# Recurrence steps of two head pairs and 128 tokens in place of one pair and 256

## The chip, the cores and the metric

The kernel runs on one core of a Trainium2 chip. The metric is the device time of one execution in microseconds (us), lower is better. The core has five engines that run side by side, each through its own instructions in order: PE (TensorE, matrix products), DVE (VectorE), ACT (ScalarE), POOL (GpSimd) and SP (SyncE, which here only issues DMAs). A matrix product needs a weight load ahead of it; the profile lists those as PEld.

## What is computed

Two layers of a decoder over 1024 tokens of width 1024. The even layer is an S5 state space model beside differential attention, the odd layer is RWKV-7 time mixing, and each layer ends with a SwiGLU feed-forward network (FFN). The change is in the RWKV-7 part alone:

```python
def rwkv7_recurrence(r, decay, k, v, kk, a):   # 16 heads of 64, 1024 tokens
    def step(state, inp):                      # state: 64 x 64 per head
        r_t, w_t, k_t, v_t, kk_t, b_t = inp
        sa = jnp.einsum('bhvk,bhk->bhv', state, -kk_t)
        state = (state * w_t[:, :, None, :] + sa[..., None] * b_t[:, :, None, :]
                 + v_t[..., None] * k_t[:, :, None, :])
        return state, jnp.einsum('bhvk,bhk->bhv', state, r_t)
    xs = (r, decay, k, v, kk, kk * a)          # along the tokens
    _, ys = lax.scan(step, s0, xs)
...
r = xr @ w_r;  k = xk @ w_k;  v = xv @ w_v     # 1024 x 1024 each
a = jax.nn.sigmoid(a0 + (xa @ a1) @ a2)
y = group_norm(rwkv7_recurrence(...)) + bonus
return (y * g) @ w_o
```

## The kernel before

The tokens are cut into two blocks of 512. For each block `rwkv_proj` computes k, r and v and puts them into DRAM (`kd`, one plane of 128 channels, so two heads, per head pair j = 0 to 7). `rwkv_algebra` then does the recurrence of the block in 16 steps of one head pair and TR = 256 tokens, and `rwkv_wo` multiplies by `w_o`. A step's 256 tokens are CR = 4 chunks of 64. Inside a chunk the token by token recurrence is replaced by products of 64 x 64 matrices, so that only the state (64 x 64 per head) goes from chunk to chunk.

A step goes through four stages, each a Python generator that yields between pieces of its work. `rwkv_prep` loads k, r, v (tiles `ks`, `rr`, `RV`), makes decays and keys from them (`pz` and `pa` are two small products with low-rank weights `wa2`, `FS` and `AR` its results) and ends with eight products `pA` that DVE masks into `AT`, `ZB` and `AR`. `rwkv_inv` inverts a triangular matrix per chunk by doubling, with PE and DVE in turn (`X`, `XE`, `QE`, `XF`), which gives `TT`. `rwkv_rec` is the recurrence over the chunks. `rwkv_out` normalises, multiplies with the gate and stores `z` to DRAM (`zd`).

`lockstep` runs four stages of four successive steps together: in each round every stage goes on by one yield, in the order out, rec, inv, prep. I call one run of `lockstep` a superstep; a block has 19. `weave` puts the FFN of another block between the rounds as filler: `RATE` = 2 times three products of 128 x 512 (L466, tiles `pg`, `pu`, `pd`) after every round. The order on PE is the order in which the code is written. The order on the other engines is set by a scheduler that simulates the kernel when it is built.

In `rwkv_rec` each chunk has three phases that hang on one another, and one yield stands between two of them. Phase one: PE multiplies with the state (`pR`, L1651, and the first half of the output, `pY`, L1653), DVE copies the result from PSUM (`Pb`, L1657). Phase two: one product with `TT` (L1660), ACT copies one half of it and DVE the other into `XU` (L1661, L1662). Phase three: PE makes the state's increment (L1666) and the rest of the output (L1668), DVE updates the state (L1673). So a superstep has twelve phases one after the other, and with its boundary 13 rounds.

The state itself stays in `Hc` between steps. The steps go over the pairs first, then over the tokens, so a pair's state is needed again eight steps later.

Of the kernel before, what the change touches and what calls it, by code (L numbers as in the profile page):

```python
# [12 lines left out]
AF = mybir.ActivationFunctionType  # L13
# [133 lines left out]
class Trunk:  # L147
# [1258 lines left out]
    def rwkv_prep(self, q, j, st):  # L1406


        nc = self.nc
        ap, pr, vec = self.ap, self.pr, self.vec  # L1410
        v, g_, s_ = nc.vector, nc.gpsimd, nc.scalar
        sl = slice(j * P, (j + 1) * P)
        tok = slice(q * TR, (q + 1) * TR)
        tw, ta = (a[:, (q * TR) % TB : (q * TR) % TB + TR] for a in (self.tw, self.ta))
# [3 lines left out]
        def t(tag, bufs=1, shape=None):  # L1418
            return ap.tile(shape or [P, TR], F32, tag=tag, name=self.nm(tag), bufs=bufs)
# [11 lines left out]
        nc.tensor.matmul(pz, lhsT=wa2, rhs=tw, start=True, stop=True)  # L1431
# [3 lines left out]
        s_.activation(lwt, pz, AF.Tanh, bias=vec[:, 0, j : j + 1], scale=0.5)  # L1435
# [20 lines left out]
        v.scalar_tensor_tensor(kk, ks, self.col("od_k_k", j), rn, op0=M, op1=M)  # L1456
# [4 lines left out]
        s_.activation(fk, at, AF.Identity, bias=vec[:, 2, j : j + 1], scale=vec[:, 3, j : j + 1])  # L1461
# [28 lines left out]
        AT, ZB = t("AT", 2, [P, CR, 64]), self.ZB[(8 * q + j) % 3]  # L1490
# [39 lines left out]
    def rwkv_inv(self, q, j, st):  # L1530
# [95 lines left out]
        for h in range(2):  # L1626
            s_.copy(XH[h][rows[h], 0, :], self.Hc[rows[h], j, :])
# [3 lines left out]
    def rwkv_rec(self, q, j, st):  # L1631
# [12 lines left out]
        def pt(tag, shape, bufs):  # L1644
            return pr.tile(shape, F32, tag=tag, name=self.nm("p" + tag), bufs=bufs)

        py = pt("Y", [P, CR, 64], 1)
        for c in range(CR):
            pp = pt("R", [P, 64], 1)
            for h in range(2):  # L1650
                te.matmul(pp[rows[h], :], lhsT=AR[h][:, c, 0:64], rhs=XH[h][:, c, :], start=True, stop=True)  # L1651
            for h in range(2):
                te.matmul(  # L1653
                    py[rows[h], c, :], lhsT=XH[h][:, c, :], rhs=AR[h][:, c, 64:128], start=True, stop=False, skip_group_check=True
                )
# [15 lines left out]
            for h in range(2):
                dst = XH[h][rows[h], c + 1, :] if c < CR - 1 else Hc[rows[h], j, :]
                v.scalar_tensor_tensor(dst, XH[h][rows[h], c, :], wc[rows[h], c : c + 1], ph[rows[h], :], op0=M, op1=AD)  # L1673
            if c < CR - 1:
                yield
# [4 lines left out]
    def rwkv_out(self, q, j, st):  # L1680
# [3 lines left out]
        sg = self.sg[:, (q * TR) % TB : (q * TR) % TB + TR]  # L1684
# [27 lines left out]
        te.matmul(pg, lhsT=g2w, rhs=sg, start=True, stop=True)  # L1712
        z = bo
        v.tensor_tensor(z, y1, pg, op=M)
        nc.sync.dma_start(self.zd[j][:, q * TR : (q + 1) * TR], z)
        yield

    def run(self):
# [46 lines left out]
        if mix1:  # L1765
            self.close(self.cq)
            self.mix1_open()
            drain(self.some(ps["v"], 16))
# [8 lines left out]
            drain(self.some(ps1["v"], 16))  # L1777
# [86 lines left out]
```

## Time and profile before

| | |
|---|---|
| median of 3 runs | 3177.56 us (3169.1 to 3178.48) |
| profiled execution, its own time | 3189.24 us |
| its span, first to last instruction | 3187.3 us |
| mean granted TensorE clock | 0.965 of 2.4 GHz |
| PE busy | 2976.2 us, 93% of the span |
| PEld / DVE / ACT / POOL busy | 71% / 60% / 37% / 28% |
| algebra of block 0, inside | 1264 to 1690 us |
| algebra of block 1, inside | 2110 to 2540 us |

The profile is of one execution, whose time lies a little above the median of the three timed runs. Lines such as L1666 are those of the kernel before. Products overlap in PE's pipeline, so the cost of one product in a series is the distance between the starts of two successive ones and not its own duration. One product in 32-bit floats shows as two matmul records; a row of "x4" is two products then. The filler's products show as one record each, about 0.23 us from start to start.

### The profile page before, as it was taken

The page shows a single profiled execution, that of the slowest core. Times are in us where ns is not written, and L with a number is a line of the kernel's source. Part 1 is how long each engine was busy: PE and PEld are TensorE (multiplying, and loading weights), DVE is VectorE, ACT ScalarE, POOL GpSimd, SP SyncE. Part 2 cuts the span into 40 slices and gives each one's busy share as a digit, 9 for nine tenths or more (in the row PEclk, how much of TensorE's full clock was granted, in tenths as well). Part 3 has the DMA queues.
Part 4 walks back from the last instruction along what each step waited for, and adds up shares of the span by engine and source line. Part 5 has one row for each costly group of instructions (what it writes and reads, how often), then busy time and mean ns, then how long its engine had stood idle before and what let it go on. Part 6 is the DMA issues. An engine that isn't in the chain of part 4 may idle for free.

```text
span 3187.3 us, 50746 instructions
## 1 busy us (share of the span) xinstructions
PE 2976.2 (93%) x19326; PEld 2250.0 (71%) x19326; DVE 1921.7 (60%) x3982; ACT 1193.9 (37%) x2446; POOL 889.5 (28%) x1007
## 2 busy tenths in 40 slices
PE   4879989999999998999999999989999999999999
PEld 1678866776777766677666777666776677777777
DVE  7744645555674645777777545467777874434443
ACT  3212334333223644444444345544444443322222
POOL 6562402000110302344434342024344444200000
PEclk7989978999999999999999999999999999999999
DMA  6853221223573444212222244522222213533332
GB/s 242 213 134 67 69 71 53 80 73 105 179 232 113 156 146 126 71 56 77 74 67 80 81 148 136 155 85 75 70 60 81 75 59 93 167 90 93 96 103 93
DMA packets 489857, 338.39 MB, mean 106 GB/s; under 512 B 44280, under 2 KB 451088, under 8 KB 488592
## 3 DMA queue, kind: packets, MB, share of 16 engines
q1 hardware_dynamic: 474288, 304.75, 32.2%
q0 software_dynamic: 7632, 25.68, 2.6%
q10 hardware_dynamic: 7696, 4.74, 0.6%
q8 instruction: 153, 2.51, 0.3%
q14 instruction: 88, 0.72, 0.1%
HBM read 292.63 MB, written 42.47 MB: 105 GB/s over the span
## 4 chain that ended last, share of the span: by engine, by line
PE 72%; DVE 12%; issue 6%; DMA 5%; ACT 3%; POOL 2%; SPq 0%; ACTq 0%; DVEq 0%; POOLq 0%
PE pg L466 13%; PE pu L466 13%; PE pd L466 12%; PE pkrv L466 8%; PE pout L466 5%; PE pq L466 3%; PE sps L1001 3%; DMA mwt<-in_w_ada 2%; PE po L1044 1%; ACT whi L449 1%; PE pR L1666 1%; PE pA L1592 1%; PE pR L1651 1%; PE pA L1495 1%; DVE wlo L450 1%
## 5 line engine op out<-in xcount | busy, mean ns | idle before, releaser
L449 ACT CAST whi<-wraw 128x1024 fp32r<-128x1024 f32 (+2 forms) x472 | 401.9, 852 | 887.7 <-PE pg L466 186.3
L466 PE MATMUL pd<-dd,whi 128*128 128x512 f32 x1408 | 463.3, 410 | 14.8 <-DVE x L534 10.7
L450 DVE TENSOR_TENSOR wlo<-wraw,whi 128x1024 fp32r<-128x1024 f32 (+2 forms) x288 | 296.1, 1029 | 271.9 <-ACT whi L449 255.4
L450 POOL TENSOR_TENSOR wlo<-wraw,whi 128x1024 fp32r<-128x1024 f32 (+2 forms) x184 | 326.0, 1773 | 461.5 <-ACT whi L449 420.1
L466 PE MATMUL pg<-fhi,whi 128*128 128x512 f32 x704 | 301.5, 428 | 13.0 <-DVE sg L521 10.8
L466 PEld LDWEIGHTS pd<-dd,whi 128*128 128x128 f32 x1408 | 254.0, 189 | 80.6 <-ACT whi L449 19.3
L466 PE MATMUL pu<-fhi,whi 128*128 128x512 f32 x704 | 295.4, 420 | 1.4 <-ACT ev L1365 0.8
L466 PE MATMUL pg<-fhi,wlo 128*128 128x512 f32 x704 | 283.4, 403 | 6.3 <-DVE wlo L450 6.3
L466 PE MATMUL pu<-fhi,wlo 128*128 128x512 f32 x704 | 279.1, 396 | 3.7 <-POOL wlo L450 2.2
L466 PE MATMUL pg<-flo,whi 128*128 128x512 f32 x704 | 281.7, 400 | 0.0
L466 PE MATMUL pd<-dd,wlo 128*128 128x512 f32 x704 | 279.4, 397 | 2.1 <-DVE oss L1053 0.9
L466 PE MATMUL pu<-flo,whi 128*128 128x512 f32 x704 | 277.7, 394 | 0.0
L534 DVE SCALAR_TENSOR_TENSOR x<-pd,mod,x 128x512 f32<-128x512 f32 x192 | 143.4, 747 | 122.9 <-PE pd L466 121.9
L466 PE MATMUL pkrv<-xh,whi 128*128 128x512 f32 x384 | 165.4, 431 | 12.3 <-ACT ev L1365 6.4
L466 PEld LDWEIGHTS pg<-fhi,whi 128*128 128x128 f32 x704 | 135.2, 192 | 47.2 <-DVE sg L521 12.0
L466 PEld LDWEIGHTS pg<-fhi,wlo 128*128 128x128 f32 x704 | 135.1, 192 | 40.3 <-DVE wlo L450 8.7
L466 PEld LDWEIGHTS pd<-dd,wlo 128*128 128x128 f32 x704 | 133.0, 189 | 38.8 <-DVE wlo L450 3.8
L466 PEld LDWEIGHTS pu<-fhi,whi 128*128 128x128 f32 x704 | 132.9, 189 | 36.3 <-issue 2.4
L466 PEld LDWEIGHTS pu<-fhi,wlo 128*128 128x128 f32 x704 | 132.6, 188 | 35.7 <-POOL wlo L450 3.0
L466 PE MATMUL pkrv<-xh,wlo 128*128 128x512 f32 x384 | 154.6, 403 | 1.3 <-DVE wlo L450 1.3
L466 PE MATMUL pkrv<-xl,whi 128*128 128x512 f32 x384 | 154.4, 402 | 0.0
L466 PEld LDWEIGHTS pg<-flo,whi 128*128 128x128 f32 x704 | 135.3, 192 | 25.3
(460 smaller groups left out, 6084.1 us busy)
## 6 DMA issues: line engine op xcount, KB each, us to landing
wraw<-in_ffn_w_gate SPq DMA_DIRECT2D x88, 512.0 KB, 3.7
wraw<-in_ffn_w_up SPq DMA_DIRECT2D x88, 512.0 KB, 3.8
wraw<-in_ffn_w_down SPq DMA_DIRECT2D x128, 256.0 KB, 2.7
mwt<-in_w_ada POOLq DMA_DIRECT2D x48, 512.0 KB, 5.4
mwt<-in_w_ada SPq DMA_DIRECT2D x32, 512.0 KB, 5.4
wraw<-in_ffn_w_down SPq DMA_DIRECT2D x64, 192.0 KB, 2.5
kd<-ev SPq DMA_DIRECT2D x48, 256.0 KB, 2.0
xs<-x SPq DMA_DIRECT2D x8, 1024.0 KB, 6.3
```

What stands on the lines that cost most here:

```text
L449: nc.scalar.copy(hi, raw)
L450: (eng or nc.vector).tensor_tensor(lo, raw, hi.bitcast(F32), op=ALU.subtract)
L466: nc.tensor.matmul(out, lhsT=w(k), rhs=x(k), start=first and i == 0, stop=last and i == n - 1)
L534: nc.vector.scalar_tensor_tensor(x[:, n, :], pd, gate[:, n : n + 1], x[:, n, :], op0=ALU.mult, op1=ALU.add)
L1001: nc.tensor.matmul(sp[:, c0 : c0 + n], lhsT=qT[r : r + 64, hd, o : o + P], rhs=kT[r : r + 64, hd % 2, c0 : c0 + n], start=True, stop=not l ...
L1044: nc.tensor.matmul(po, lhsT=wt[:, j - j0, :], rhs=vt[:, j, P * (hd % 2) : P * (hd % 2) + P], start=(j == 0), stop=(j == i))
L1495: nc.tensor.matmul(pas[h][:, c, :], lhsT=FS[rows[h], c, :], rhs=AR[h][rows[h], c, :], start=True, stop=True)
L1592: te.matmul(px[32 * g : 32 * g + 32], lhsT=XF[:, g, :], rhs=QE[:, g], start=True, stop=True)
L1651: te.matmul(pp[rows[h], :], lhsT=AR[h][:, c, 0:64], rhs=XH[h][:, c, :], start=True, stop=True)
L1666: te.matmul(ph[rows[h], :], lhsT=BE[:, c, rows[h]], rhs=XU[h][:, c, :], start=True, stop=True)
```

## The change

One step takes two neighbouring pairs (2j and 2j + 1) and 128 tokens in place of one pair and 256. A step still has four chunks of 64 tokens, now two of each pair, and all tiles keep their size of 256 columns (`u = 2 e + c` is chunk c of pair e). The recurrence goes in two rounds over c, and each round carries a chunk of both pairs in every phase. Between two phases stand two yields in place of one (`self.wait(2)`).

What depends on the pair (weights and per-channel factors) is done once for each of the two pairs on 128 columns: the products `pz`, `pa`, `pbn` and `pg`, four activations in `rwkv_prep` and one in `rwkv_out`, the product `kk` on DVE and `Brk` on POOL. The loads of k, r, v and the store of `z` take two planes in rows of 512 bytes in place of one in rows of 1 KB. `rr` and `wa2` have one buffer in place of two. A pair's state comes back after four steps.

```diff
@@ rwkv_algebra
-                    q, j = divmod(16 * b + s - d, 8)
+                    q, j = divmod(16 * b + s - d, 4)
@@ rwkv_prep
-        ks, rr, RV = t("ks"), t("rr", 2), t("RV", 4, [P, 2, TR])
+        pairs = [(2 * j + e, slice(e * P, (e + 1) * P)) for e in range(2)]
+        ks, rr, RV = t("ks"), t("rr"), t("RV", 4, [P, 2, TR])
         for d, dst in ((0, ks), (1, rr), (2, RV[:, 1, :])):
-            nc.sync.dma_start(dst, self.kd[d, j][:, tok])
-        wa2 = t("wa2", 2, [P, P])
+            nc.sync.dma_start(e2(dst), self.kd[d, 2 * j : 2 * j + 2].rearrange("e p t -> p e t")[:, :, tok])
+        wa2 = t("wa2", 1, [P, 2 * P])
...
-        nc.tensor.matmul(pz, lhsT=wa2, rhs=tw, start=True, stop=True)
+        for _, o in pairs:
+            nc.tensor.matmul(pz[:, o], lhsT=wa2[:, o], rhs=tw, start=True, stop=True)
...
-        s_.activation(lwt, pz, AF.Tanh, bias=vec[:, 0, j : j + 1], scale=0.5)
+        for i, o in pairs:
+            s_.activation(lwt[:, o], pz[:, o], AF.Tanh, bias=vec[:, 0, i : i + 1], scale=0.5)
...
@@ rwkv_inv
-            s_.copy(XH[h][rows[h], 0, :], self.Hc[rows[h], j, :])
+            s_.copy(XH[h][rows[h], 0::2, :], self.Hc[rows[h], 2 * j : 2 * j + 2, :])
@@ rwkv_rec
+        def units(c):
+            return [(e, 2 * e + c, h) for e in range(2) for h in range(2)]
...
-        for c in range(CR):
-            pp = pt("R", [P, 64], 1)
-            for h in range(2):
-                te.matmul(pp[rows[h], :], lhsT=AR[h][:, c, 0:64], rhs=XH[h][:, c, :], start=True, stop=True)
+        for c in range(2):
+            pp = pt("R", [P, 2, 64], 1)
+            for e, u, h in units(c):
+                te.matmul(pp[rows[h], e, :], lhsT=AR[h][:, u, 0:64], rhs=XH[h][:, u, :], start=True, stop=True)
...
-            Pb = t("Pb", [P, 64], 2)
+            Pb = t("Pb", [P, 2, 64])
             v.tensor_copy(Pb, pp)
-            yield
-            pu = pt("R", [P, 64], 1)
-            te.matmul(pu, lhsT=TT[:, c, :], rhs=Pb, start=True, stop=True)
-            s_.copy(XU[0][rows[0], c, :], pu[rows[0], :])
-            v.tensor_copy(XU[1][rows[1], c, :], pu[rows[1], :])
-            yield
+            yield from self.wait(2)
+            pu = pt("R", [P, 2, 64], 1)
+            for e in range(2):
+                te.matmul(pu[:, e, :], lhsT=TT[:, 2 * e + c, :], rhs=Pb[:, e, :], start=True, stop=True)
+            s_.copy(XU[0][rows[0], c::2, :], pu[rows[0]])
+            v.tensor_copy(XU[1][rows[1], c::2, :], pu[rows[1]])
+            yield from self.wait(2)
...
@@ run
-            drain(self.some(ps["v"], 16))
+            drain(self.some(ps["v"], 20))
```

The first place is on PE, late in a superstep of block 0. Before, a round holds the product of phase two (L1660) and the next one its phase three (L1666, L1668), with six products of filler between:

```order
L1660 MATMUL pR_16353<-Pb_16312,TT_10249 128x64
L1622 MATMUL pA_16357<-QE_16316,XF_16323 32x128 x2
L466 MATMUL pg_16349<-fhi_10338,whi_16345 128x512
L466 MATMUL pg_16349<-flo_10340,whi_16345 128x512
L466 MATMUL pg_16349<-fhi_10338,wlo_16346 128x512
L466 MATMUL pg_16349<-fhi_10338,whi_16345 128x512
L466 MATMUL pg_16349<-flo_10340,whi_16345 128x512
L466 MATMUL pg_16349<-fhi_10338,wlo_16346 128x512
L1666 MATMUL pR_16373<-XU_3377_15391,BE_15605 64x64
L1666 MATMUL pR_16373<-XU_3378_15392,BE_15605 64x64
L1668 MATMUL pY_15956<-ZB_10247,XU_3377_15391 64x64
L1668 MATMUL pY_15956<-ZB_10247,XU_3378_15392 64x64
```

Now phase three (L1685, L1687 of the new code) carries four units, and the round ahead of it ends with the last product `pA` of the preparation (L1508), while phase two stands a round earlier still, out of sight above the first row:

```order
L1508 MATMUL pA_16648<-AR_3610_16583,FS_16577 128x128
L466 MATMUL pg_16552<-fhi_10359,whi_16548 128x512
L466 MATMUL pg_16552<-flo_10361,whi_16548 128x512
L466 MATMUL pg_16552<-fhi_10359,wlo_16549 128x512
L466 MATMUL pg_16552<-fhi_10359,whi_16548 128x512
L466 MATMUL pg_16552<-flo_10361,whi_16548 128x512
L466 MATMUL pg_16552<-fhi_10359,wlo_16549 128x512
L1685 MATMUL pR_16666<-XU_3396_15743,BE_15941 64x64
L1685 MATMUL pR_16666<-XU_3397_15744,BE_15941 64x64
L1685 MATMUL pR_16666<-XU_3396_15743,BE_15941 64x64
L1685 MATMUL pR_16666<-XU_3397_15744,BE_15941 64x64
L1687 MATMUL pY_16283<-ZB_10245,XU_3396_15743 64x64
```

What moved: phases two and three of a chunk lie twelve filler products and one more group of other products apart, where it was six.

The second place is on DVE at the same point. Before, the copy `XU` (L1662), for which phase three waits, stands behind the six masks of the preparation (L1498), one FFN update and `AC`:

```order
L1657 COPY Pb_21999<-pR_21994 128x64
L1612 TENSOR_TENSOR QE_22003<-pA_22001,cstt 128x256
L1498 TENSOR_TENSOR AT_22012<-pA_22013,cstt 64x256
L1498 TENSOR_TENSOR ZB_10245<-pA_22013,cstt 64x256
L1498 TENSOR_TENSOR AR_4976_21930<-pA_22013,cstt 64x512
L1498 TENSOR_TENSOR AT_22012<-pA_22014,cstt 64x256
L1498 TENSOR_TENSOR ZB_10245<-pA_22014,cstt 64x256
L1498 TENSOR_TENSOR AR_4977_21931<-pA_22014,cstt 64x512
L534 SCALAR_TENSOR_TENSOR x_4365_19583<-pd_21990,mod_119,x_4365_19583 128x512
L1568 SCALAR_TENSOR_TENSOR AC_22105<-AT_22012,cstt 128x128
L1662 COPY XU_4756_21091<-pR_22032 64x64
L1625 COPY TT_10248<-pA_22036 32x4x32
```

Now the copy (L1681) stands ahead of the masks (L1511), and with the inversion's `X` behind the burst of the preparation (`y`, `ksq`, `AR`, `FS`: L1468 to L1485):

```order
L1601 TENSOR_TENSOR QE_21004<-pA_20999,cstt 128x256
L1468 SCALAR_TENSOR_TENSOR y_4600_21006<-ks_20737,vc_103,hbc_20978 128x128 x2
L1471 SCALAR_TENSOR_TENSOR ksq_21009<-at_20830,y_4600_21006 128x256
L1485 SCALAR_TENSOR_TENSOR AR_4605_21021<-y_4600_21006,Wx_20795 64x4x64
L1485 SCALAR_TENSOR_TENSOR AR_4606_21022<-y_4600_21006,Wx_20795 64x4x64
L1481 SCALAR_TENSOR_TENSOR FS_21016<-ksq_21009,L_20788 64x4x64 x2
L1606 TENSOR_TENSOR X_20730<-X_20730,pA_21041 128x4x16
L1681 COPY XU_4400_20223<-pR_21036 64x2x64
L1615 TENSOR_TENSOR XE_21047<-X_20730,cstt 128x256
L1617 STREAM_TRANSPOSE X_4611_21049<-X_20730 128x128
L1625 TENSOR_TENSOR QE_21076<-pA_21074,cstt 128x256
L1511 TENSOR_TENSOR AT_21085<-pA_21086,cstt 64x256
```

What moved: `XU` from behind the masks to a place ahead of them, one copy for two units.

## Rows read from the trace of the kernel before

**Rows 1.** By stretch: length; busy PE, PEld, DVE, ACT, POOL; clock; DMA share, GB/s.

```profile
1264.00:1690.00 426.00, 404.03 (x3644) 294.78 (x3644) 320.47 (x824) 181.90 (x473) 179.35 (x178) 0.99 0.24 70
...
2110.00:2540.00 430.00, 407.64 (x3670) 297.82 (x3670) 323.05 (x829) 183.11 (x475) 179.36 (x179) 0.99 0.23 69
```

**Rows 2.** PE's waits, whole span: us in total, times, longest us.

```profile
PE pR L1666 <- DVE XU L1662: 26.3, 30, 2.8
...
PE pA L1585 <- DVE Pb L1657: 7.1, 9, 1.5
...
PE pA L1585 <- DVE XE L1577: 3.0, 9, 0.7
```

**Rows 3.** PE in time: start, us, line, product, records [idle before, its end].

```profile
1383.42 0.48 PE L1666 MATMUL pR<-XU,BE 128*64 128x64 f32 x4 [2.76 <-DVE XU L1662]
...
1469.27 0.34 PE L1666 MATMUL pR<-XU,BE 128*64 128x64 f32 x4 [0.69 <-DVE XU L1662]
...
1613.71 0.34 PE L1666 MATMUL pR<-XU,BE 128*64 128x64 f32 x4 [1.63 <-DVE XU L1662]
```

**Rows 4.** DVE in order of time, a superstep's end.

```profile
1424.66 0.68 DVE L1498 TENSOR_TENSOR AR<-pA,cstt 64x512 f32<-64x512 f32 x1
...
1425.93 0.33 DVE L1568 SCALAR_TENSOR_TENSOR AC<-AT,cstt 128x128 f32<-128x128 f32 x1
1426.29 0.23 DVE L1662 COPY XU<-pR 64x64 f32<-64x64 f32 x1
...
1429.04 1.13 DVE L1577 TENSOR_TENSOR XE<-X,cstt 128x256 f32<-128x256 f32 x1
```

**Rows 5.** PE in order of time, 1418 to 1435 us.

```profile
1418.39 0.71 PE L1483 MATMUL pv<-cstt,RV 128*128 128x128 f32 x4
1418.86 0.71 PE L466 MATMUL pd<-dd,whi 128*128 128x512 f32 x2
1419.41 0.40 PE L466 MATMUL pd<-dd,wlo 128*128 128x512 f32 x1
...
1423.91 0.33 PE L1660 MATMUL pR<-Pb,TT 128*128 128x64 f32 x2
1424.17 0.41 PE L1622 MATMUL pA<-QE,XF 128*32 128x128 f32 x4
...
1426.58 0.34 PE L1666 MATMUL pR<-XU,BE 128*64 128x64 f32 x4 [0.40 <-DVE XU L1662]
1426.74 0.29 PE L1668 MATMUL pY<-ZB,XU 128*64 128x64 f32 x4
1426.96 0.73 PE L466 MATMUL pd<-dd,whi 128*128 128x512 f32 x2
1427.53 0.40 PE L466 MATMUL pd<-dd,wlo 128*128 128x512 f32 x1
1427.76 0.63 PE L466 MATMUL pd<-dd,whi 128*128 128x512 f32 x2
...
1429.63 0.39 PE L466 MATMUL pd<-dd,wlo 128*128 128x512 f32 x1
1429.94 0.34 PE L1651 MATMUL pR<-XH,AR 128*64 128x64 f32 x4
...
1433.31 0.70 PE L1446 MATMUL pa<-lta,wa 128*128 128x256 f32 x2
1433.66 0.81 PE L466 MATMUL pd<-dd,whi 128*128 128x512 f32 x2
1434.31 0.39 PE L466 MATMUL pd<-dd,wlo 128*128 128x512 f32 x1
```

**Rows 6.** PE's weight loads in order of time, the loads of one of these groups.

```profile
1418.39 0.52 PEld L1483 LDWEIGHTS pv<-cstt,RV 128*128 128x128 f32 x4
```

**Rows 7.** DVE's groups of instructions, 1264 to 1690 us: busy us, mean ns.

```profile
L1662 DVE COPY XU<-pR 64x64 f32<-64x64 f32 x47 | 10.7, 228 | 2.0 <-ACT XU L1661 0.5
...
L1673 DVE SCALAR_TENSOR_TENSOR Hc<-XH,wc,pR 64x64 f32<-64x64 f32 x22 | 6.1, 279 | 0.8
```

More of the change, by code (lines that the diff above doesn't have):

```diff
@@ L1445, in rwkv_prep @@
         pa = pr.tile([P, TR], F32, tag="k", name=self.nm("pa"))
-        nc.tensor.matmul(pa, lhsT=wa2, rhs=ta, start=True, stop=True)
+        for _, o in pairs:
+            nc.tensor.matmul(pa[:, o], lhsT=wa2[:, o], rhs=ta, start=True, stop=True)
         yield
         at = t("at")
-        s_.activation(at, pa, AF.Tanh, bias=vec[:, 1, j : j + 1], scale=0.5)
+        for i, o in pairs:
+            s_.activation(at[:, o], pa[:, o], AF.Tanh, bias=vec[:, 1, i : i + 1], scale=0.5)
         ksq = t("ksq")
-        s_.activation(ksq, ks, AF.Square, scale=self.col("od_k_k", j))
+        for i, o in pairs:
+            s_.activation(ksq[:, o], ks[:, o], AF.Square, scale=self.col("od_k_k", i))
         yield
@@ L1455, in rwkv_prep @@
         kk = t("y1")
-        v.scalar_tensor_tensor(kk, ks, self.col("od_k_k", j), rn, op0=M, op1=M)
+        for i, o in pairs:
+            v.scalar_tensor_tensor(kk[:, o], ks[:, o], self.col("od_k_k", i), rn[:, o], op0=M, op1=M)
         bt = t("ksq")
@@ L1460, in rwkv_prep @@
         fk = t("kr")
-        s_.activation(fk, at, AF.Identity, bias=vec[:, 2, j : j + 1], scale=vec[:, 3, j : j + 1])
+        for i, o in pairs:
+            s_.activation(fk[:, o], at[:, o], AF.Identity, bias=vec[:, 2, i : i + 1], scale=vec[:, 3, i : i + 1])
         k2 = t("lwt")
@@ L1488, in rwkv_prep @@
         yield
-        AT, ZB = t("AT", 2, [P, CR, 64]), self.ZB[(8 * q + j) % 3]
+        AT, ZB = t("AT", 2, [P, CR, 64]), self.ZB[(4 * q + j) % 3]
         msk = self.cst("tri").rearrange("p (o n) -> p o n", o=1)
@@ L1668, in rwkv_rec @@
+            s_.copy(XU[0][rows[0], c::2, :], pu[rows[0]])
+            v.tensor_copy(XU[1][rows[1], c::2, :], pu[rows[1]])
+            yield from self.wait(2)
+            ph = pt("R", [P, 2, 64], 1)
+            for e, u, h in units(c):
+                te.matmul(ph[rows[h], e, :], lhsT=BE[:, u, rows[h]], rhs=XU[h][:, u, :], start=True, stop=True)
+            for e, u, h in units(c):
                 te.matmul(
-                    py[rows[h], c, :], lhsT=XU[h][:, c, :], rhs=ZB[:, h, c, :], start=False, stop=True, skip_group_check=True
+                    py[rows[h], u, :], lhsT=XU[h][:, u, :], rhs=ZB[:, h, u, :], start=False, stop=True, skip_group_check=True
@@ L1670, in rwkv_rec @@
                 )
[L1671 to L1675, printed above, removed]
+            for e, u, h in units(c):
+                dst = Hc[rows[h], 2 * j + e, :] if c else XH[h][rows[h], u + 1, :]
+                v.scalar_tensor_tensor(dst, XH[h][rows[h], u, :], wc[rows[h], u : u + 1], ph[rows[h], e, :], op0=M, op1=AD)
@@ L1676, in rwkv_rec @@
+            if not c:
+                yield from self.wait(2)
         st["ys"] = ys = t("ys", [P, TR])
@@ L1683, in rwkv_out @@
         ap, pr = self.ap, self.pr
-        sg = self.sg[:, (q * TR) % TB : (q * TR) % TB + TR]
+        sg = self.sg[:, (q * P) % TB : (q * P) % TB + P]
+        pairs = [(2 * j + e, slice(e * P, (e + 1) * P)) for e in range(2)]
         v, g_, s_, te = nc.vector, nc.gpsimd, nc.scalar, nc.tensor
@@ L1703, in rwkv_out @@
         v.tensor_tensor(y1, ys, rb, op=M)
-        s_.activation(y1, y1, AF.Identity, bias=self.col("od_ln_b", j), scale=self.col("od_ln_g", j))
+        for i, o in pairs:
+            s_.activation(y1[:, o], y1[:, o], AF.Identity, bias=self.col("od_ln_b", i), scale=self.col("od_ln_g", i))
         pbn = pr.tile([P, TR], F32, tag="y", name=self.nm("pR"))
-        te.matmul(pbn, lhsT=Brk, rhs=RV[:, 0, :], start=True, stop=True)
+        for _, o in pairs:
+            te.matmul(pbn[:, o], lhsT=Brk[:, o], rhs=RV[:, 0, o], start=True, stop=True)
         bo = yq
@@ L1711, in rwkv_out @@
         pg = pr.tile([P, TR], F32, tag="y", name=self.nm("pR"))
-        te.matmul(pg, lhsT=g2w, rhs=sg, start=True, stop=True)
+        for _, o in pairs:
+            te.matmul(pg[:, o], lhsT=g2w[:, o], rhs=sg, start=True, stop=True)
         z = bo
         v.tensor_tensor(z, y1, pg, op=M)
-        nc.sync.dma_start(self.zd[j][:, q * TR : (q + 1) * TR], z)
+        nc.sync.dma_start(
+            self.zd[2 * j : 2 * j + 2].rearrange("e p t -> p e t")[:, :, q * P : (q + 1) * P], z.rearrange("p (e t) -> p e t", e=2)
+        )
         yield
@@ L1776, in run @@
             fs, fs1 = {}, {}
-            drain(self.some(ps1["v"], 16))
+            drain(self.some(ps1["v"], 20))
             if ffn1:
```

25 lines of the change are left out of this document (12 added, 13 removed).

## The prediction

> **What bounds the kernel now.** I first read the busy time by stretch [rows 1]. In the algebra of both blocks PE is busy 404.03 of 426 us and 407.64 of 430 us, at a granted clock of 0.99 (the 2.4 GHz level). PE is the bound there, and it is idle for 22 us in each stretch, 44 us in all. DVE is second with 320.47 us, 75%. ACT (181.90 us) and POOL (179.35 us) have room, and so have the DMAs (share 0.24). So the change can gain in two ways only: fewer or cheaper products on PE, and less idle time of PE. The filler is only shifted: six filler products fewer stand in each superstep (72 in place of 78 in PE's order) and follow after the algebra instead.
>
> Next I read who PE waits for [rows 2]. The longest wait of the kernel is the one that the change is about: L1666, phase three of a chunk, waits for the DVE copy `XU`, 26.3 us in 30 waits. Two waits of the inversion follow (L1585 behind `Pb` and `XE`): 7.1 + 3.0 = 10.1 us in 18 waits. The first of them is named after `Pb`, but L1585 does not read `Pb`; `XE` stands next to it in DVE's queue.
>
> Then I looked at where in the superstep the 30 waits lie, by their distance from `pz`, which opens it. There are four places, and the same ones come back in both blocks: 5 to 6 us after `pz` (8 waits, 4.9 us, such as the one at 1469.27), 14.7 us (2 waits, 3.3 us, the one at 1613.71), 21 to 23 us (8 waits, 10.9 us, the longest of them 2.76 us at 1383.42) and 29 to 33 us (12 waits, 7.2 us, such as 0.40 us at 1426.58) [rows 3, 5]. The last place shows the cause: DVE ends its masks at 1425.34, does `AC`, and copies `XU` only at 1426.29, and L1666 starts at 1426.58 [rows 4, 5]. PE waits because a copy of 0.23 us stands in line behind long work of another stage. At 21 to 23 us it is the burst of the preparation (`y`, `ksq`, `AR`, `FS`).
>
> **The change part by part: PE's own work.** The number of products in the recurrence is the same. What changes is how they are grouped, and I price that by distances between starts [rows 5].
>
> Merged groups: four records of L1666 last 0.16 us until L1668 (1426.58 to 1426.74), a group of the same shape, while L1668 lasts 0.22 us until a line of another shape follows (1426.74 to 1426.96). So a group that is followed by its own kind costs 0.06 us less. Phases one and three each put two former groups of two lines into one: 3 x 0.16 + 0.22 = 0.70 us in place of 2 x 0.38 = 0.76. A step has four such merges: 4 x 0.06 = 0.24 us.
>
> Phase two: L1660 takes 0.26 us until the next line (1423.91 to 1424.17). Two in a row can save between nothing and half of one, 0.13 us. No row shows two in a row; I take the 0.06 of the merge above, which is the nearest. Two pairs a step: 0.12 us.
>
> One round less: a superstep has 12 rounds in place of 13, so one change less from filler to other products and back. Going in, the last filler product takes 0.31 us (1429.63 to 1429.94) in place of 0.23 (1427.53 to 1427.76): 0.08. Coming out, two filler products take 0.57 us (1426.96 to 1427.53) in place of 0.46: 0.11. Together 0.19 us.
>
> Split products: `pz`, `pa`, `pbn` and `pg` become two products of 128 columns with a weight load each. The trace has this pair in another place: L1483 is two products of 128 columns with two sets of weights. From its start to the second filler record it takes 1.02 us (1418.39 to 1419.41), and L1446, one product of 256 columns, takes 1.00 us by the same measure (1433.31 to 1434.31). So 0.02 us each, four per step: 0.08 us.
>
> That is 0.24 + 0.12 + 0.19 - 0.08 = 0.47 us a step, and with 32 steps 15 us less. The bounds: if only the missing round counts (32 x 0.19 = 6 us) and each of the 128 splits costs one load of L1483, 0.52 / 4 = 0.13 us [rows 6], which is 17 us, the part turns into a loss of 11 us; if phase two saves all of 0.13 twice a step, the gain is 0.14 x 32 = 4 us larger, 19 us.
>
> A rule speaks against this part. In the Trainium skill, TensorE: Matmul & The Clock Gate, section LDWEIGHTS (loading the stationary operand), a weight load takes about its columns divided by 1.2 in nanoseconds, whatever the rows, and in section The mechanism it overlaps with running products only where the row group differs. Here 4 more products of two loads each in 32 steps are 256 more loads of 128 columns; by that rule, as an estimate, they would cost 27 us, and the sum below would shrink from 30 to 3 us. The rows of L1483 and L1446 above speak against it: the additional load costs 0.02 us there.
>
> **The waits.** Behind the masks (7.2 us) the wait goes: in DVE's new order `XU` stands ahead of the masks, and phase three comes two rounds after phase two. At 5 to 6 us (4.9 us) it goes too, as there is a whole round more. At 14.7 us (3.3 us) I count half, 1.6 us. At 21 to 23 us (10.9 us) I count half, 5.5 us: the recurrence no longer waits, but the inversion's product in the same round needs `QE` or `X` from the same DVE queue, and in one of the two orders that I see in turn `QE` stands behind the burst. Together 19 us less.
>
> Against it: every second round loses the 0.38 us of recurrence products that covered the inversion, and the inversion still has one round between its phases. If half of its 18 waits grow by 0.38 us, that is 3.4 us; I take 4. So 15 us less in waits, between 36 us less (26.3 + 10.1, all gone) and 8 us more (nothing gained, each of 18 waits longer by 0.4).
>
> What costs nothing: DVE saves half of the `Pb` and `XU` copies (0.228 us each, [rows 7]) and has one `kk` more. ACT has five more activations and half of the `XU` copies less, at 43% busy. POOL has one `Brk` more at 42%. Rows of 512 bytes double the pieces of the `kd` loads; `ks` is free to load after `kk` and `k2` of the step before, some rounds ahead of its use. `rr` and `wa2` with one buffer make SP wait for POOL's `RV` and PE's `pa` of the step before; behind them in SP's queue stand filler weights. In SP's order their loads now stand at the place where `ks` and `RV` of the same step stood, so no new wait lasts longer than those that SP already has. If that cover is gone, filler weights come late, and PE would wait in L466.
>
> **The sum.** 15 + 15 = 30 us less. Of the profiled execution, 3189.24 us (span 3187.3 us), that makes 3159. It lies 0.4% above the median of the runs, and the waits and distances are the same in both, so I take the 30 us from the median: 3177.56 - 30 = 3148 us.
>
> **The rivals.** First, the waits only change their name: DVE is 75% busy, the bursts are as long as before, and PE stops at the inversion instead (`QE` behind the burst, `XE` behind `FS`). For it: the inversion's 18 waits show that it has no slack in places. Against it: the masks are now behind `XU` and ahead of nothing that PE needs in that round. Then only PE's work counts, 15 us: 3163 us.
>
> Second, all of the waits of rows 2 go, because with one copy for two units and no update between them DVE's queue is short where it matters: 15 + 36 = 51 us, 3127 us.
>
> Third, the change doesn't do what it says on PE: the additional loads stand on the path. Four loads of L1483 take 0.52 us [rows 6], 0.13 each, and 256 of them 33 us. With the 30 us gained that is 3181 us, no change. The rule on weight loads named above points the same way.
>
> Fourth, slower: the chain from the masks to the next superstep's first products. DVE goes from the masks over `AC`, the state updates, `X` and its transpose to `XE`, which ends at 1430.17; the products that need it stand ahead of L1446 at 1433.31 [rows 4, 5], about 3 us later. The change takes a round out of this stretch (six filler products and a crossing, 1.6 us) and puts two more `Hc` updates into DVE's queue (2 x 0.28 us, [rows 7]): 2.2 us less slack. In the superstep shown 0.8 us is left. It decides where the slack before was under 2.2 us: with 0.7 us in each of some 28 full supersteps PE would wait 1.5 x 28 = 42 us, and 3148 + 42 = 3190 us. Against it: `XE` alone took 1.13 us there, and the rows of such a wait are short now.
>
> **How the numbers follow.** Forecast, 3148 us: 0.53. Waits change their name, 3163: 0.20. All waits go, 3127: 0.10. Loads on the path, 3181: 0.07. The chain behind the masks, 3190: 0.10. About 0.3%, 9.5 us, is what a measurement of this kernel can tell from no change; so faster begins below 3168. Faster: nearly all of the forecast, 0.16 of the first rival and all of the second, 0.78. Same: the rest of the first, most of the third, 0.12. Slower 0.10. The range leaves out 0.1 at either end: 3126 to 3174 us.
>
> **What would show it.** Right: L1685 (once L1666) waits for `XU` for under 5 us; the full supersteps are shorter by about 2.5 us, of which 1.4 us are shifted filler; PE's idle time in the algebra falls from 44 to about 30 us; two products of `pz` and `pa` cost what one did. Wrong: waits of L1598 and L1605 (the inversion) of 20 us and more, a wait at L1598 early in each superstep, or gaps of L466 behind filler weights.

## The result, and the profile after

The changed kernel takes 3224.28 us (median of 4 runs, 3220.45 to 3227.83); the kernel before takes 3174.05 us beside it. The ratio is 1.0146 with an interval of 1.0120 to 1.0171. The forecast was 3148 us, with a range of 3126 to 3174. By the ratio the change makes the kernel slower by some 46 us; the measured time lies outside the range, and the forecast missed the sign.

The profiled execution took 3227.83 us, its span is 3226.0 us. In the new code the inversion's lines are L1598 (once L1585, reads `XE`), L1605 (once L1592, reads `QE`) and L1628 (the step behind, reads the second `XE`). Phase one is L1668 and L1671, phase two L1679, phase three L1685 and L1687. The first line to read is PE's busy time in the page of the changed kernel: engine, busy us, share of the span, instructions.

```profile
PE 2953.4 (92%) x19582; PEld 2268.7 (70%) x19582; DVE 1972.0 (61%) x3886; ACT 1217.7 (38%) x2542; POOL 908.4 (28%) x1039
```

Before, PE was busy 2976.2 us and DVE 1921.7 us. PE is busy 22.8 us less although the span is 38.7 us longer, so it is idle 61.5 us longer. DVE is busy 50.3 us longer with 96 instructions fewer. That second pair of numbers already points at the answer: DVE's instructions got longer on average. PE's waits say who pays (whole span of the changed kernel: us in total, times, longest us).

```profile
PE pA L1598 <- DVE XE L1590: 54.5, 30, 3.1
PE pA L1605 <- DVE QE L1601: 28.5, 16, 2.5
...
PE pA L1628 <- DVE XE L1615: 9.7, 16, 0.9
...
PE pA L1605 <- ACT XU L1680: 3.4, 4, 2.1
...
PE pA L1605 <- ACT kr L1474: 2.9, 4, 0.7
```

The wait that the change is about is gone: no wait of L1685 for `XU` is left, where L1666 had 26.3 us [rows 2]. In its place the inversion waits. The five lines make 99.0 us, the three of before 36.4 us [rows 2], so 63 us more, about the 61.5 us of idle time; less the 22.8 us of PE's busy time that is 40 us, about the 38.7 us by which the span grew. By stretch (length; busy PE, PEld, DVE, ACT, POOL; granted clock; DMA share, GB/s), the answer to [rows 1] is:

```profile
1260.00:1690.00 430.00, 385.49 (x3691) 291.46 (x3691) 339.03 (x788) 185.01 (x505) 177.31 (x184) 0.97 0.23 68
2140.00:2570.00 430.00, 386.63 (x3705) 292.88 (x3704) 340.27 (x792) 187.65 (x514) 175.85 (x182) 0.97 0.23 66
```

PE is idle for 44 us in each stretch in place of 22, and the granted clock has gone from 0.99 to 0.97. Now one superstep in time. On DVE (start, us, line, operation, tiles, shape):

```profile
1462.87 2.52 DVE L1590 TENSOR_TENSOR XE<-X,cstt 128x256 f32<-128x256 f32 x1
...
1470.44 0.43 DVE L1590 TENSOR_TENSOR XE<-X,cstt 128x256 f32<-128x256 f32 x1
...
1477.12 2.97 DVE L1485 SCALAR_TENSOR_TENSOR AR<-y,Wx 64x256 f32<-64x256 f32 x2
...
1481.01 0.42 DVE L1601 TENSOR_TENSOR QE<-pA,cstt 128x256 f32<-128x256 f32 x1
...
1489.82 2.48 DVE L1583 TENSOR_TENSOR X<-AC,cstt 128x128 f32<-128x128 f32 x1
...
1492.94 0.28 DVE L1583 TENSOR_TENSOR X<-X,cstt 128x128 f32<-128x128 f32 x1
```

The same instruction on the same shape takes 0.43 us or 2.52 us (`XE`), and `X` 0.28 or 2.48 us. POOL in the same superstep:

```profile
1462.78 2.34 POOL L450 TENSOR_TENSOR wlo<-wraw,whi 128x1024 fp32r<-128x1024 f32 x1 [0.96 <-ACT whi L449]
...
1477.43 2.37 POOL L450 TENSOR_TENSOR wlo<-wraw,whi 128x1024 fp32r<-128x1024 f32 x1 [3.31 <-ACT whi L449]
...
1489.79 2.37 POOL L450 TENSOR_TENSOR wlo<-wraw,whi 128x1024 fp32r<-128x1024 f32 x1 [7.69 <-ACT whi L449]
...
1500.16 2.34 POOL L450 TENSOR_TENSOR wlo<-wraw,whi 128x1024 fp32r<-128x1024 f32 x1 [0.96 <-ACT whi L449]
1514.78 2.47 POOL L450 TENSOR_TENSOR wlo<-wraw,whi 128x1024 fp32r<-128x1024 f32 x1 [3.30 <-ACT whi L449]
1526.63 1.30 POOL L450 TENSOR_TENSOR wlo<-wraw,whi 128x512 fp32r<-128x512 f32 x1 [5.82 <-ACT whi L449]
```

L450 computes the low half `wlo` of a filler weight tile on POOL. Each of the three long rows on DVE (`AR` is two instructions in one row) starts within 0.4 us of a `wlo` and ends 0.1 to 0.3 us after it (1465.39 after 1465.12, 1480.09 after 1479.80, 1492.30 after 2.37 us from 1489.79). `pz` opens the superstep at 1454.8, and the next one at 1491.44: the three `wlo` start 8.0, 22.6 and 35.0 us after the first `pz` and 8.7, 23.3 and 35.2 us after the second, so the same places are hit again (the last of the six is a tile of 512 columns and runs for 1.30 us). On PE in the same superstep (in square brackets the idle time before and what ended it):

```profile
1462.34 0.27 PE L1593 MATMUL pA<-ident,X 128*128 128x128 f32 x1
1465.54 0.32 PE L1598 MATMUL pA<-XE,AC 128*32 128x64 f32 x8 [2.93 <-DVE XE L1590]
...
1474.46 0.45 PE L1668 MATMUL pR<-XH,AR 128*64 128x64 f32 x8
1474.74 0.40 PE L1671 MATMUL pY<-AR,XH 128*64 128x64 f32 x8
1475.07 0.32 PE L1605 MATMUL pA<-QE,XF 128*32 128x64 f32 x8
...
1481.58 0.32 PE L1605 MATMUL pA<-QE,XF 128*32 128x64 f32 x8 [2.10 <-DVE QE L1601]
...
1491.44 0.71 PE L1438 MATMUL pz<-ltw,wa 128*128 128x128 f32 x4
...
1492.45 0.40 PE L466 MATMUL pg<-fhi,wlo 128*128 128x512 f32 x1
```

The held `XE` becomes a wait of 2.93 us at L1598. The held `AR` puts `QE` behind it in DVE's queue, and that becomes a wait of 2.10 us at L1605. `XU` is there in time for L1685, which starts without a wait. A third thing follows the long wait. By stretches of 4 us (columns as above) the clock reads:

```profile
1462.00:1466.00 4.00, 1.07 (x29) 0.68 (x28) 3.91 (x5) 0.91 (x2) 2.34 (x1) 1.00 0.11 33
1466.00:1470.00 4.00, 4.00 (x33) 2.91 (x34) 2.60 (x9) 1.50 (x3) 1.41 (x2) 0.63 0.47 135
```

It is 1.00 (the 2.4 GHz level) in the gap, and 0.63 behind it: about three quarters of these 4 us at the 1.2 GHz level. PE is fully busy there and does 4 x 0.63 = 2.5 us of work, so some 1.5 us are lost besides the 2.93. They are booked as busy time of PE, not as a wait.

### The profile page after: what moved, and what is told of

Same layout as the page of the kernel before. It is cut to its first block, busy times and chain, and to the rows that moved or that the text cites. A ratio compares the mean times of both kernels' runs of the same rounds, so it can differ in the third digit from the quotient of the medians.

```text
span 3226.0 us, 51402 instructions
## 1 busy us (share of the span) xinstructions
PE 2953.4 (92%) x19582; PEld 2268.7 (70%) x19582; DVE 1972.0 (61%) x3886; ACT 1217.7 (38%) x2542; POOL 908.4 (28%) x1039
## 4 chain that ended last, share of the span: by engine, by line
PE 68%; DVE 19%; DMA 5%; ACT 3%; issue 3%; POOL 1%; SPq 0%; ACTq 0%; DVEq 0%; POOLq 0%
PE pg L466 13%; PE pu L466 12%; PE pd L466 12%; PE pkrv L466 8%; PE pout L466 5%; PE pq L466 4%; PE sps L1001 2%; DMA mwt<-in_w_ada 2%; DVE XE L1590 2%; DVE FS L1481 2%; DVE X L1583 2%; DVE AR L1485 1%; PE pA L1508 1%; PE po L1044 1%; DVE AR L1511 1%
## 5 line engine op out<-in xcount | busy, mean ns | idle before, releaser
L466 PE MATMUL pd<-dd,whi 128*128 128x512 f32 x1408 | 462.3, 410 | 12.4 <-DVE x L534 7.8
L450 DVE TENSOR_TENSOR wlo<-wraw,whi 128x1024 fp32r<-128x1024 f32 (+2 forms) x288 | 296.6, 1030 | 289.2 <-ACT whi L449 280.6
L450 POOL TENSOR_TENSOR wlo<-wraw,whi 128x1024 fp32r<-128x1024 f32 (+2 forms) x184 | 326.9, 1779 | 464.5 <-ACT whi L449 447.3
L466 PE MATMUL pg<-fhi,whi 128*128 128x512 f32 x704 | 301.8, 429 | 12.7 <-DVE sg L521 10.1
```

What stands on the lines that cost most here:

```text
L450: (eng or nc.vector).tensor_tensor(lo, raw, hi.bitcast(F32), op=ALU.subtract)
L466: nc.tensor.matmul(out, lhsT=w(k), rhs=x(k), start=first and i == 0, stop=last and i == n - 1)
```

## The experiments

**The theory:** a DVE instruction with both operands in SBUF is held while POOL's `wlo` runs, and the new superstep puts `wlo` on instructions that PE waits for, in the same places each time. The expectations call this theory A, and theory C where they ask about the same places coming back (the "lock": 24 filler units are three weight tiles of 8 units). **The rival:** the shorter superstep is slower by itself: with one round less the inversion has less cover, or less filler stands between its steps, whatever POOL does; this is theory B.

**POOL's `wlo` left out**, in the changed kernel and in the kernel before. The filler's products with `wlo` then read `whi`, so the low half of these weights is missing from the result; the number of products stays.

```
         hi = self.wp.tile(shape, F32R, tag="whi", name=self.nm("whi"))
         nc.scalar.copy(hi, raw)
+        if eng is not None:
+            return hi, hi
```

> The changed kernel without POOL's subtraction wlo in the FFN: the products that read wlo read whi instead, so the low half of the filler's weights is left out; PE's work, the loads and the casts stay. Theory A (POOL's wlo holds DVE instructions that read two SBUF operands, and in the changed kernel it holds those of the inversion): the waits at L1598 behind XE (54.5 us) fall under 15 us, XE, AR, X and ksq go back to their plain 0.42 to 0.45 us and X to 0.29, and the time falls from 3224 by 50 us or more, to 3175 or less. Theory B (one round less a superstep: DVE has too little time whatever POOL does): the waits stay over 60 us in all, the time stays above 3205.

> The kernel before, with the same part left out (the FFN's wlo on POOL replaced by whi). Theory A: a smaller gain than in the changed kernel, 5 to 25 us (the stretched instructions were mostly dd, for which PE does not wait), so 3150 to 3170, and the changed kernel without wlo is then the faster of the two by 5 to 25 us, as its products take less of PE. Theory B: the difference of about 50 us between the two kernels stays.

Measured: 3094.84 us for the changed kernel (ratio to before 0.9750, interval 0.9723 to 0.9777) and 3122.60 us for the one of before (0.9841, 0.9811 to 0.9870). Without `wlo` the change makes the kernel 28 us faster; with it, 46 us slower. The changed kernel did what theory A said. The kernel before did not: it gained 53 us (3175.45 us beside it) where 5 to 25 were expected, so `wlo` costs it more than a stretched `dd`. DVE's groups in the algebra of both blocks, 1200 to 2720 us (count | busy us, mean ns | idle), without `wlo`:

```profile
L1592 DVE TENSOR_TENSOR XE<-X,cstt 128x256 f32<-128x256 f32 x128 | 54.1, 423 | 3.0
L1603 DVE TENSOR_TENSOR QE<-pA,cstt 128x256 f32<-128x256 f32 x128 | 54.1, 423 | 13.0 <-PE pA L1600 11.4
...
L527 DVE TENSOR_TENSOR dd<-hd,dd 128x512 fp32r<-128x512 f32 x44 | 30.3, 688 | 10.2 <-ACT dd L526 9.9
...
L1487 DVE SCALAR_TENSOR_TENSOR AR<-y,Wx 64x256 f32<-64x256 f32 x64 | 26.6, 416 | 0.4
...
L1473 DVE SCALAR_TENSOR_TENSOR ksq<-at,y 128x256 f32<-128x256 f32 x32 | 13.4, 419 | 0.3
L1585 DVE TENSOR_TENSOR X<-AC,cstt 128x128 f32<-128x128 f32 x32 | 9.4, 292 | 0.9
```

The same groups in the changed kernel:

```profile
L1590 DVE TENSOR_TENSOR XE<-X,cstt 128x256 f32<-128x256 f32 x128 | 89.7, 701 | 2.9
L1485 DVE SCALAR_TENSOR_TENSOR AR<-y,Wx 64x256 f32<-64x256 f32 x64 | 56.7, 885 | 0.4
L1601 DVE TENSOR_TENSOR QE<-pA,cstt 128x256 f32<-128x256 f32 x128 | 53.9, 421 | 13.7 <-PE pA L1598 12.4
L1583 DVE TENSOR_TENSOR X<-AC,cstt 128x128 f32<-128x128 f32 x32 | 53.8, 1682 | 1.0
...
L525 DVE TENSOR_TENSOR dd<-hd,dd 128x512 fp32r<-128x512 f32 x41 | 38.0, 927 | 8.9 <-ACT dd L524 8.7
L1471 DVE SCALAR_TENSOR_TENSOR ksq<-at,y 128x256 f32<-128x256 f32 x32 | 27.7, 865 | 0.6
```

And in the kernel before:

```profile
L1577 DVE TENSOR_TENSOR XE<-X,cstt 128x256 f32<-128x256 f32 x128 | 68.0, 531 | 3.1
L525 DVE TENSOR_TENSOR dd<-hd,dd 128x512 fp32r<-128x512 f32 x44 | 65.5, 1489 | 11.0 <-ACT dd L524 10.7
...
L1472 DVE SCALAR_TENSOR_TENSOR AR<-y,Wx 64x256 f32<-64x256 f32 x64 | 29.4, 459 | 0.5
...
L1570 DVE TENSOR_TENSOR X<-AC,cstt 128x128 f32<-128x128 f32 x32 | 14.2, 444 | 0.8
```

Mean by mean against the first fence, the hold on the four groups that the inversion needs or stands behind (`XE`, `X`, `AR`, `ksq`) is 35.6 + 44.5 + 30.0 + 14.3 = 124 us in the changed kernel and 13.8 + 4.9 + 2.8 + 0 = 21.5 us in the one before. On `dd`, a step of the filler, it is the other way: 9.8 us after, 35.2 us before. `QE`, which reads PSUM, keeps its 421 ns in the changed kernel. So both kernels pay the hold, the old one for the larger part on `dd`. PE's waits at L1598 and L1605 (here L1600 and L1607) without `wlo`:

```profile
PE pA L1607 <- DVE QE L1603: 6.6, 10, 1.0
PE pA L1600 <- DVE XE L1592: 5.8, 22, 0.5
```

12.4 us in place of the 83.0 us of L1598 and L1605. The rival can't explain that: the rounds and the filler's pace are the same in both. In the kernel before, the wait at L1666 (here L1668) for `XU` falls as well, from 26.3 us in 30 waits to 9.9 us in 18:

```profile
PE pR L1668 <- DVE XU L1664: 9.9, 18, 0.9
```

So most of the wait that the change was made for was the hold too. The longest, 2.76 us at 1383.42 [rows 3], stands behind two `FS` that a `wlo` held on DVE (first row DVE, second POOL; two `FS` take 0.85 us elsewhere):

```profile
1379.13 2.92 DVE L1468 SCALAR_TENSOR_TENSOR FS<-ksq,L 64x256 f32<-64x256 f32 x2
1378.82 2.52 POOL L450 TENSOR_TENSOR wlo<-wraw,whi 128x1024 fp32r<-128x1024 f32 x1 [4.17 <-ACT whi L449]
```

**The number of filler units in a superstep.** A round takes `RATE` units; the changed kernel has 12 rounds and 24 units in a superstep, and the one before 13 and 26. First run: a thirteenth round.

```
+        yield
         st["ys"] = ys = t("ys", [P, TR])
```

> The changed kernel with one more yield at the end of the recurrence, so 13 rounds in a superstep and 78 filler products as before. Theory A: the stretched instructions stay, at other places; 3195 to 3225. Theory B: the time that was taken from DVE is back, the waits at L1598 and L1605 fall from 83 to under 40 us, 3160 to 3185.

Then 12 rounds with 26 units, as below, and with 25 (a rate of 25/12), and the kernel before with 24 units in its 13 rounds (24/13).

```
-RATE = 2.0
+RATE = 13.0 / 6.0
```

> The changed kernel with RATE = 13/6 in place of 2: 12 rounds, but 78 filler products in a superstep, as before. Theory A: 3195 to 3225, the waits move a little with the places of POOL's wlo. Theory B: as with 13 rounds, 3160 to 3185.

> The changed kernel with RATE = 25/12: 25 units a superstep, no multiple of 8, only one unit more than the changed kernel. Theory C: unlocked, so near the 3149 of RATE 13/6, 3140 to 3185. Theory B (the loss follows the number of filler units in a superstep, 24 gives 3224 and 26 gives 3149): half way, 3180 to 3195.

> The kernel before with RATE = 24/13, so 24 units or three weight tiles a superstep in its 13 rounds. Theory C: it is locked too, and its time moves by 10 us or more, to the side that the place of wlo decides. Theory B (fewer filler products a superstep leave DVE too little time): slower than before, 3190 to 3215, as in the changed kernel. If the pace doesn't matter: 3168 to 3184.

Measured: 26 units 3149.21 us (0.9916, 0.9888 to 0.9943), 25 units 3158.15 us (0.9939, 0.9919 to 0.9959), the thirteenth round 3187.18 us (1.0034, 1.0015 to 1.0054), before with 24 units 3226.23 us (1.0155, 1.0122 to 1.0188). One unit more per superstep takes 66 us off the changed kernel, and two units less put 47 us on the one before (3178.74 us beside it). `wlo` runs in all of them and falls in other places, but the filler between two steps changes with it, so these runs alone don't part theory and rival. With 25 units the time lies where theory C had it; with 26 it lies below what either theory gave, and the kernel before with 24 above what the rival gave. The thirteenth round lay between what the two theories gave: its waits are 35.7 us at L1598 and 17.5 us at L1605, up to 3.3 us long, against 24.0 and 17.1 us with `RATE` 13/6. That is 12 us of the 38 us between them. PE's busy time has most of the rest, 2944.2 against 2916.2 us for the same 19582 instructions, at a granted clock of 0.97 against 1.00 in the algebra of the first block: a cost of the lower clock, which the theory had not had in it.

**The place alone.** The filler starts 2, 4 (below) or 6 units ahead of the algebra; rounds, units and instructions stay.

```
-            drain(weave(self.rwkv_algebra(0), fill, lambda: self.rate))
+            drain(self.some(fill, 4), weave(self.rwkv_algebra(0), fill, lambda: self.rate))
...
-                drain(weave(self.rwkv_algebra(1), fill, lambda: self.rate))
+                drain(self.some(fill, 4), weave(self.rwkv_algebra(1), fill, lambda: self.rate))
```

> The changed kernel with two filler units ahead. Known so far: 0 units 3224, 4 units 3143, 6 units 3149. Theory C: again another place of wlo, the same in each superstep with weight tiles of 1024 columns, so the time lies anywhere from 3140 to 3240 and follows the waits at L1598 and L1605. Theory B (the pace alone): 3215 to 3230, with 4 and 6 units unexplained.

> The changed kernel with four filler units (12 products) done ahead of each block's algebra, so that all weight tiles of the filler, and with them POOL's wlo, come four units (half a weight tile) later in the superstep; RATE 2, 12 rounds and all else as changed. Theory C (lock: 12 rounds x 2 = 24 units are exactly three weight tiles of 8, so wlo falls on the same DVE instructions superstep after superstep): the time moves by 15 us or more from 3224, to either side, and the stretched instructions are others, the same in most supersteps. Theory B (the missing round itself costs): 3215 to 3230.

> The same with six units ahead. Theory C: again another time than 3224 and than with four units, by 10 us or more, with other instructions stretched. Theory B: 3215 to 3230.

Measured: 3124.14 us (0.9837, 0.9817 to 0.9857), 3142.81 us (0.9885, 0.9858 to 0.9912) and 3149.42 us (0.9914, 0.9884 to 0.9945). With the same superstep and the same 24 units the changed kernel takes 3124 or 3224 us, by nothing but the place of the filler. The rival, that the short superstep is slow by itself, falls for the changed kernel. How much a place costs was not foreseen: 2 units ahead came out below the 3140 to 3240 us expected, and 6 units ahead only 7 us from 4 units, where 10 or more were expected. The wait at L1598 with 2 units ahead:

```profile
PE pA L1598 <- DVE XE L1590: 23.8, 33, 1.1
```

and DVE's groups there:

```profile
L1590 DVE TENSOR_TENSOR XE<-X,cstt 128x256 f32<-128x256 f32 x128 | 98.6, 771 | 2.4
...
L1583 DVE TENSOR_TENSOR X<-AC,cstt 128x128 f32<-128x128 f32 x32 | 9.4, 292 | 1.0
```

`X` is free of the hold, but `XE` is held even longer than in the changed kernel (mean 771 ns against 701), and yet PE waits 31 us less at L1598 and never over 1.1 us there. So for this wait it isn't the sum of the holds on `XE` that counts but which instance is hit. In the superstep above PE had issued L1593 at 1462.34, before the held `XE` began, and had nothing else until L1598; here a held `XE` runs from 1469.26 to 1471.63, L1593 starts only at 1470.74, and PE waits 0.77 us. With these short waits the clock stays at 1.00 in the algebra of both blocks, and PE is busy 2920.0 us, 33 us less than in the changed kernel for as many instructions.

The kernel before was moved in the same way, with its own 26 units and with 24.

> The kernel before with four filler units ahead, at its own RATE of 2 and 13 rounds, 26 units a superstep. Theory C: 26 is no multiple of 8, wlo drifts through all places of the superstep either way, so the time stays within 15 us of before, 3163 to 3192. If the place of the filler matters in the same way without a lock: it moves by 25 us or more.

> The kernel before with RATE = 24/13 and four filler units ahead of each algebra. Theory C (only the place of wlo in the locked superstep makes the slower pace dear): the 66.5 us of waits at L1666 behind XU fall to under 35 us and the time falls from 3226 to 3160 to 3195. Theory B (fewer filler products a superstep cost by themselves): 3215 to 3235.

Measured: 3207.82 us (1.0104, 1.0072 to 1.0137) and 3248.20 us (1.0224, 1.0188 to 1.0260). Both missed the expectation. With 26 units the place was expected to matter little, since it drifts from superstep to superstep; it costs 32 us (waits at L1666 of 41.6 us). So a place that repeats isn't needed for a loss. With 24 units the move was expected to help and cost another 22 us. Its waits are 62.5 us at L1666 for `XU`, against 66.5 us unmoved. In the two traces 60.8 and 64.4 us of them come within 1.5 us behind a DVE instruction that took over 0.3 us longer than the short instances of its kind while a `wlo` ran (by the same count 20.0 of the 26.3 us in the kernel before). Unmoved it is mostly the `FS` of the preparation (1008 ns on the mean, 420 without `wlo`), moved it is for half of the time `AC` (1012 ns, 337 without); first row unmoved, second row moved:

```profile
L1468 DVE SCALAR_TENSOR_TENSOR FS<-ksq,L 64x256 f32<-64x256 f32 x64 | 64.5, 1008 | 1.3
L1568 DVE SCALAR_TENSOR_TENSOR AC<-AT,cstt 128x128 f32<-128x128 f32 x32 | 32.4, 1012 | 0.0
```

So in the old kernel both places put the hold in front of `XU`. What 24 units would cost there without any hold was not run and stays open.

**`wlo` in pieces.** The same subtraction in pieces of 2 planes (256 columns), in the changed kernel, in the one before, and in the changed kernel with 4 units ahead or with `RATE` 13/6.

```
+            for k in range(0, shape[1], 2):
+                eng.tensor_tensor(
+                    lo[:, k : min(k + 2, shape[1]), :], raw[:, k : min(k + 2, shape[1]), :], hi[:, k : min(k + 2, shape[1]), :].bitcast(F32), op=ALU.subtract
+                )
```

> The changed kernel with POOL's wlo in pieces of two planes (256 columns) in place of one instruction of 1024. Theory A (DVE is held until the running POOL instruction ends): DVE can go on after a piece of 0.6 us, so the stretched instructions shrink from about 2.5 to 1.1 us, the waits at L1598 fall from 54.5 to under 25 us, 3150 to 3180. If POOL's pieces hold DVE one after another as one long instruction does: 3215 to 3230.

> The kernel before with POOL's wlo in pieces of two planes. Theory A: it gains less than the changed kernel did by the same edit (88 us), 10 to 35 us, so 3140 to 3168, since its filler drifted against the superstep; the changed kernel with pieces (3136) stays the faster by 5 to 30 us, the gain by PE's work and the waits at XU.

> The changed kernel with pieces and with four units ahead, the two edits that each undid the loss. If both act on the same thing, the second brings little: 3115 to 3140. It may be the fastest version. Not below 3100, since without any wlo on POOL the changed kernel took 3095.

> The changed kernel with pieces and RATE = 13/6, which unlocks the filler from the superstep: 3110 to 3145, within 15 us of the one with four units ahead, as with pieces the place matters little.

Measured: 3135.71 us (0.9868, 0.9835 to 0.9902) for the changed kernel, 3155.19 us (0.9928, 0.9902 to 0.9953) for the one before, 3126.53 us (0.9842, 0.9806 to 0.9878) and 3115.31 us (0.9798, 0.9765 to 0.9832) for the two combinations, both inside what was expected. A piece takes 0.80 us in place of 2.4, and the hold shrinks with it: the longest `XE` in the changed kernel is then 1.05 us in place of 2.53. The pieces give the changed kernel 89 us, more than the 44 to 74 expected, and the old one 24. With them the change itself is worth 3155 - 3136 = 19 us, as the expectation for the old kernel had it. The last combination is the fastest kernel of this study with the whole computation, 2.0% below the kernel before. Its two longest algebra waits:

```profile
PE pA L1604 <- DVE XE L1596: 16.3, 26, 1.2
...
PE pA L1611 <- DVE QE L1607: 13.5, 19, 1.6
```

Some 30 us are left at the same two places; POOL is busy for longer (987.1 us against 908.4), 32% of the span.

## Why the prediction was wrong

**What bounds the kernel.** Right: PE is the bound. The waits at `XU` were found in the right places, but not their cause: they were put down to the order in DVE's queue, and 26.3 us became 9.9 us when nothing but `wlo` was left out. DVE was judged by its share, 75% [rows 1], and not by what its instructions would take alone. That share had the hold in it (DVE's busy time in the whole program falls from 1921.7 to 1830.1 us without `wlo`).

**PE's own work, 15 us less.** The sign was right, the size too small. The merged group of phase one takes 1474.46 to 1475.07 = 0.61 us for 16 records; 0.70 was predicted, and 0.76 for the two groups of before. The split `pz` takes 1491.44 to 1492.45 = 1.01 us up to the start of the third filler product behind it; L1446 took 1.00 by the same measure [rows 5]. PE's busy time for the whole program compares best where no long wait lowers the clock: with `wlo` in pieces it is 2910.5 us after and 2949.1 before, 39 us less; without `wlo` 2924.5 and 2946.1, 22 us less (a low value: the first of these two ran its first 800 us, ahead of the algebra, at a clock of 0.90 against 0.93). So the term was 22 to 39 us. In the changed kernel itself PE was busy 33 us longer than in the run with 2 units ahead, so as much was lost again at the lower clock. The lower bound of this part counted 128 loads where the third rival counted 256; with 256 it would have been a loss of 27 us and not 11.

**The rule on weight loads** (third rival, 3181 us): not borne out. A split product with its additional loads cost 0.01 us more where it was measured, and PE's busy time fell.

**The waits, 15 us less.** This is the step that failed. The 19 us at `XU` were too low: all 26.3 us of L1666 went, at L1685 none came. The 4 us that were set against it for the inversion were 99.0 - 10.1 = 89 us, the five lines of after against the two of the inversion in [rows 2], and the clock behind the long waits came on top. The prediction took each DVE duration as fixed and asked only for the order in the queue. The term doesn't come out without the hold either: with `wlo` left out PE is idle 173.2 us in the kernel before (span less busy time) and 178.0 us in the changed one. So the 28 us gained there come from PE's own work.

**What costs nothing.** The filler was "only shifted" and its weights were checked for SP's queue alone. Moving it moves POOL's `wlo` against DVE's instructions, and that is where the gain of 28 us turned into a loss of 46. The sign of it stood in the rows: `XE` at 1429.04 took 1.13 us [rows 4], and the text used it as an accident of that superstep. On POOL at that moment, in the trace of before:

```profile
1428.87 1.02 POOL L450 TENSOR_TENSOR wlo<-wraw,whi 128x384 fp32r<-128x384 f32 x1 [3.35 <-ACT whi L449]
```

A look at the means by shape would have shown the rest: `dd` at 1489 ns, and `XE` at 531 ns where most instances take 0.43 us.

**The rivals.** The first (waits change their name to the inversion) had the place right, and gave 3163 us because it moved the waits without lengthening them; it describes the two kernels without `wlo` best (9.9 us at `XU` before, 17.6 us at L1600, L1607 and L1630 of the inversion after). The fourth, on the slower side, named `XE` and L1598 too, by a shorter chain behind the masks; the twelve longest waits at L1598 (2.9 to 3.1 us) stand 10.7 to 11.6 us after `pz`, behind a held `XE`, and without `wlo` none there is over 0.5 us, so its mechanism is not what was measured. No rival had one engine that holds another up. Of the signs listed for wrong, "waits of L1598 and L1605 of 20 us and more" came out; two of those for right did too, L1685 without a wait for `XU` and `pz` at its old cost, and they decided nothing.

## What to carry to other kernels

Before a duration goes into a sum, compare the mean of its group with its shortest instance on the same shape; where they differ, look at what the other engines run at that moment, since a change that moves either one moves the stretch. When a change alters the length of a loop against background work that is woven into it, time it at several offsets of that work: here one kernel gave 3124 to 3224 us, more than the change is worth. A long instruction on an engine that seems idle at 28% can be cut into pieces, so that whatever it holds up is held for less. Here that gave 89 and 24 us.

## What the runs showed of the hardware

- A DVE instruction that reads two operands from SBUF stands still while a POOL `TENSOR_TENSOR` of 128x1024 runs: 0.43 us become 2.52, 0.28 become 2.48, and with POOL's instruction left out the means are 423 and 292 ns. With POOL's instruction in pieces of 0.80 us the longest `XE` of the changed kernel takes 1.05 us. `QE`, with one operand in PSUM, doesn't change (421 ns with, 423 without). POOL's own instruction keeps its 2.34 to 2.47 us. The Trainium skill, SBUF — State Buffer, section Who interferes with whom, says so: a DVE instruction with two SBUF inputs contends with a GpSimd instruction that reads SBUF, and the port pair that the two share is an exclusive lock. The trace agrees, with ends 0.1 to 0.3 us after POOL's.
- A wait of 2.93 us of PE at a granted clock of 1.00 was followed by 4 us at 0.63, and the wait of 2.10 us that ended at 1481.58 by no fall: 1.00 from 1482 to 1486. Over the program the 19582 records of the changed kernel took 33 us longer with the long waits than in the run with 2 units ahead (2953.4 against 2920.0 us).
- Two groups of small products of one shape in a row cost less than apart: the 16 records of phase one take 0.61 us, where two groups of 8 (L1666 with L1668 [rows 5]) take 2 x 0.38 us.
